# A transformer trunk on one core: new warm-up operands, the first chunk of x in halves, and weights rounded block by block in the opening

## The chip, the core and the metric

The kernel runs on one core of a Trainium2 chip. A core has a matrix engine (TensorE, PE in the profile, with its weight loads listed as PEld), three engines for other arithmetic (VectorE = DVE, ScalarE = ACT, GpSimd = POOL), an engine that mainly issues transfers (SyncE = SP), and 16 DMA engines, which move data between the chip's memory and the core's own memory. The metric is the device time of one execution in microseconds (us); a kernel's figure is the median of its runs.

## The reference

Two layers, sequence 512, width 1024, all in float32. Each layer: RMS norm, one combined input projection to 3072 columns, eight heads of stick-breaking attention and four of differential attention with rotary position, an output projection with residual add, RMS norm, and a squared-ReLU MLP of width 4096 with residual add. A final RMS norm ends it.

```python
h = rmsnorm(x, attn_norm[l])
proj = jnp.einsum('bsd,de->bse', h, w_in[l])
...
x = x + jnp.einsum('bse,ed->bsd', mixed, w_o[l])
h = rmsnorm(x, mlp_norm[l])
u = jnp.square(jax.nn.relu(jnp.einsum('bsd,df->bsf', h, w_ff1[l])))
x = x + jnp.einsum('bsf,fd->bsd', u, w_ff2[l])
```

## The kernel before

The activations lie transposed: `x` has 8 chunks (`KC`), chunk c with 128 features on the partitions and the 512 tokens along the row. The input projection's weights come in units of 128 columns, each a tile `raw` of 128x1024: 8 blocks of 128x128, block c belonging to chunk c.

Float32 accuracy is made from three products of rounded numbers. A value a is split into a rounded part and a rest, `hi` and `lo`, and a·b is taken as hi·hi + hi·lo + lo·hi. So each chunk costs three matmuls of 128x512 per unit. ACT makes the rounded part (L117 for weights, L250 for activations, there times the norm's gain), and DVE the rest (L133 and L251). The row factor 1/rms is applied later, to the results, so projections can begin before the norm is known.

The opening works on units 0 and 1 together (banks `p00` and `p01`, in the trace `p`), chunk by chunk, as the chunks of `x` and the blocks of the two weight tiles `raw0` and `raw1` arrive:

- ACT's queue fetches `begin` (L203: the gains and block 0 of `raw0`) and blocks 1 to 3 of `raw0` (L204).
- SP's queue fetches the chunks of `x` (L206) and, behind every second chunk, two blocks of `raw1` and, from chunk 4 on, two of `raw0` (L209). Later transfers reuse the completion semaphores of earlier ones: eight stand in a ring, so the ninth transfer of the program waits until the first has landed, the tenth until the second has, and so on.
- POOL fills the tile `edge` with zeros and an identity. PE runs eight warm-up matmuls of 128x512 in bf16 on the zeros (`WARM`, L223); their result is not used.
- `W.split_part(i, a, b)` rounds columns a to b of weight tile i; `make_h(c, g)` rounds chunk c. Block 0 of unit 0 is rounded on DVE (L116), all else on ACT.
- In `dense` (L785 to L803) PE works through chunk 0 with six matmuls at L792, chunk 1 with six at L796, and from chunk 2 on with the general three per unit and chunk (L300 to L302).

What runs in which order on one engine is decided when the program is built, by a scheduler that takes the code's order and its own estimate of when each operand is ready. `behind(a, b)` adds an edge: a is placed after b on its engine. Each engine then works strictly in that order, and a wait holds back all that is behind it. After the opening, four more units (`p0w`) follow on PE at once.

The lines by which the opening's rounding is ordered before the change:

```python
W.split_part(0, 0, P)
W.eager = False
opened = make_h(0, gcol("attn", 0, 0))
behind(opened[1], W.last[1])
W.split_part(1, 0, 2 * P)
...
W.split_part(0, P, 2 * P)
```

Of the kernel before, what the change touches and what calls it, by code (L numbers as in the profile page):

```python
# [9 lines left out]
F32 = mybir.dt.float32  # L10
F32R = mybir.dt.float32r
BF16 = mybir.dt.bfloat16
AF = mybir.ActivationFunctionType
# [4 lines left out]
P = 128  # L18
S = 512
# [146 lines left out]
def trunk(ctx, tc, opened, xT, w, w2, w1, gfin, lamv, cos, sin, out):  # L166
    nc = tc.nc
# [10 lines left out]
    def bank(tag, name):  # L178
        if tag == "any":
            tag = ("mm", "s", "s", "mm", "s")[turn[0] % 5]  # L180
            turn[0] += 1
        ring[0] += tag == "s"
        return ps.tile([P, 512], F32, tag=tag, name=name, bufs=banks[tag])
# [3 lines left out]
    W = _Weights(nc, w, wraw, wspl)  # L187
# [3 lines left out]
    x = cp.tile([P, KC, S], F32, tag="x", name="x")  # L191
# [7 lines left out]
    ident = edge[:, 384:512]  # L199
    lam_sm = cp.tile([P, L, 2], F32, tag="lamsm", name="lam_sm")  # L200
    lam_ex = cp.tile([P, L, 2], F32, tag="lamex", name="lam_ex")
    raws = [wraw.tile([P, 1024], F32, tag="raw", name=f"raw{i}") for i in range(2)]
    nc.scalar.dma_start(begin, opened)  # L203
    nc.scalar.dma_start(raws[0][:, P : 4 * P], w[0][:, P : 4 * P])  # L204
    for c in range(KC):
        nc.sync.dma_start(x[:, c, :], xT[c])  # L206
        if c % 2 == 0:
            for i in range(c < 4, 2):
                nc.sync.dma_start(raws[i][:, c * P : (c + 2) * P], w[i][:, c * P : (c + 2) * P])  # L209
    W.raw = dict(enumerate(raws))  # L210
    W.loaded = 2
    W.load(3)

    make_identity(nc, ident)
    mhalf = cp.tile([P, 4], F32, tag="mhalf", name="mhalf")
    nc.vector.memset(mhalf, -0.5)
    nc.gpsimd.memset(edge[:, 0:384], 0.0)
    prime = cp.tile([P, 1], F32, tag="prime", name="prime")
    nc.scalar.activation(prime, mhalf[:, 0:1], AF.Exp)
    zeros = edge.bitcast(BF16)  # L220
    pw = bank("t", "warm")
    for _ in range(WARM):
        nc.tensor.matmul(pw, zeros[:, 0:128], zeros[:, 128:640], start=True, stop=True)  # L223

    def gcol(which, l, c):
        i = {"attn": l * 8, "mlp": 16 + l * 8, "final": 32, "sub": 40 + l}[which] + c
        return g_all[:, i : i + 1]
# [18 lines left out]
            out=lo, in0=src, scalar=-1.0, in1=hi.bitcast(F32), op0=ALU.mult, op1=ALU.subtract)  # L246
        return a

    def make_h(c, g):
        a = nc.scalar.activation(h_hi[:, c, :], x[:, c, :], AF.Copy, scale=g)  # L250
        return a, nc.vector.scalar_tensor_tensor(  # L251
            out=h_lo[:, c, :], in0=x[:, c, :], scalar=g, in1=h_hi[:, c, :].bitcast(F32),
            op0=ALU.mult, op1=ALU.subtract)

    def add_sq(c, first, sqt, eng=nc.gpsimd):
# [6 lines left out]
    def behind(a, b):  # L262
        tc.add_manual_dep(a.ins, b.ins.name, mybir.DependencyInfo(
            mybir.DependencyClass.NoSync, mybir.DependencyReason.DATA), reason="order")
# [71 lines left out]
    for l in range(L):  # L336
        with ExitStack() as actx:
# [22 lines left out]
            if l == 0:  # L360
                W.eager = True
                W.split_part(0, 0, P)
                W.eager = False
                opened = make_h(0, gcol("attn", 0, 0))
                behind(opened[1], W.last[1])
                W.split_part(1, 0, 2 * P)
                for a, b in zip(W.last, opened):
                    behind(a, b)
                ahead = W.last
                W.split_part(0, P, 2 * P)  # L370
                for a, b in zip(W.last, ahead):
                    behind(a, b)
                for c in range(1, KC):
                    if c % 2 == 0:
                        for i in range(2):
                            W.split_part(i, c * P, (c + 2) * P)
                            if (c, i) == (2, 0):
                                for a, b in zip(W.last, opened):
                                    behind(a, b)
                    opened = make_h(c, gcol("attn", 0, c))  # L380
                    if c == 1:
                        for a, b in zip(opened, W.last):
                            behind(a, b)
                W.split = 2
            else:
                pts, halfway, opened = opened_by.pop()
# [399 lines left out]
            def dense(pts):  # L786
                if l == 0:
                    us = [W.next("x"), W.next("x")]
                    pts = [bank("mm", f"p{l}{i}") for i in range(2)]
                    for i, m in ((0, 0), (0, 2), (1, 0), (0, 1), (1, 1), (1, 2)):  # L790
                        a, b = wpair(us[i], 0), hpair(0)
                        nc.tensor.matmul(pts[i], a[m == 2], b[m == 1], start=m == 0, stop=False)  # L792
                    yield 6 * 0.216
                    for i, m in ((0, 0), (1, 0), (0, 2), (1, 2), (0, 1), (1, 1)):
                        a, b = wpair(us[i], 1), hpair(1)
                        nc.tensor.matmul(pts[i], a[m == 2], b[m == 1], start=False, stop=False)  # L796
                    yield 6 * 0.216
                    turns = [(c, i) for c in range(2, 5) for i in range(2)] + [(c, i) for i in range(2) for c in (5, 6, 7)]
                    for c, i in turns:
                        three(pts[i], wpair(us[i], c), hpair(c), False, c == KC - 1)  # L800
                        yield 3 * 0.216
                step, b = 2 * KC, int(ORDER[0][1])
                held = [(pts[0], "d", b, "q"), (pts[1], "d", b, "k")]  # L803
                def walk(name, kind, b, which):
                    if kind in "wu":
                        for _ in all_values() if kind == "w" else values_of(b):
                            yield None
                    else:
                        yield from block(name, "mm")

                for item in ORDER[1:]:
                    kind, b = item[0], int(item[1])
                    for which in ("qk" if kind in "ds" else "v"):
                        for pt in walk(f"p{l}{kind}{b}{which}", kind, b, which):
                            step += 1
                            if step == RA[l]:
                                rms_a(ssq, 1.0 / D, rcol, f"a{l}", last=W.product)
                            if step == RB[l]:
                                rms_b(rbc, f"a{l}", rcol)
                                nc.vector.tensor_mul(cos_t, cos_t, rbc)  # L820
                                nc.vector.tensor_mul(sin_t, sin_t, rbc)
                                for args in held:
                                    evict_d(*args)
                                held = []
                            yield 3 * 0.216
                        if kind in "ds":
                            {"s": evict_s, "d": evict_d}[kind](pt, kind, b, which)
                yield from wo(1)
# [551 lines left out]
```

## Time and profile before

| what | value |
|---|---|
| median of 3 runs | 1124.26 us (1123.91 to 1124.55) |
| the profiled execution's own time | 1124.27 us |
| its span, first instruction to last | 1122.5 us |
| PE busy | 1114.8 us, 99% of the span |
| DVE, ACT, POOL busy | 80%, 61%, 14% |

The rows shown further on have the start of an instruction and its length in us from the span's start, then engine, line, operation, tiles and shapes. In brackets stands how long its engine sat idle before it, and what ended that. `SPq` and `ACTq` rows are the issues of transfers; their length is that of the issue, not of the transfer. The lengths of matmuls are modelled and overlap, so the pace of PE is read from the distance between starts. In a row that merges several instructions (`x2`) only the first start is shown.

### The profile page before, as it was taken

To read this page: it belongs to the slowest core of one execution; us is meant where nothing else is said; L and a number is where in the kernel's file an instruction comes from. 1 tells how busy PE (TensorE), PEld (TensorE's weight loads), DVE (VectorE), ACT (ScalarE), POOL (GpSimd) and SP (SyncE) were. 2 spreads that over 40 slices of the span, in tenths; PEclk is the share of its full clock that TensorE was granted. 3 is DMA by queue.
4 is the path that set the end of the run, shared out by engine and by line. 5 is a ranking of instruction groups with operands and counts; after the bars stand their busy time and mean duration, and the time that the engine had idled before them with its cause. 6 is when DMAs were issued, how large, how long until landed. Compare 5 with 4: busy or idle time off the path is not lost.

```text
span 1122.5 us, 17199 instructions
## 1 busy us (share of the span) xinstructions
PE 1114.8 (99%) x6377; PEld 978.2 (87%) x6377; DVE 903.4 (80%) x1309; ACT 682.7 (61%) x1107; POOL 153.6 (14%) x233
## 2 busy tenths in 40 slices
PE   9999999999999999999999999999999999999997
PEld 7889889888899899899878898988888998998986
DVE  7788788798668779779877887887787787797787
ACT  6446666667558457467344566665774584674665
POOL 1001344101011001001000014430011010010010
PEclk9999999999999999999999999999999999999999
DMA  7466343268687678658325654512676786787462
GB/s 249 137 191 184 112 133 114 73 220 232 172 217 169 182 200 185 189 134 211 109 75 148 197 146 130 168 59 76 209 175 183 202 189 175 184 185 206 113 132 94
DMA packets 61043, 181.25 MB, mean 161 GB/s; under 512 B 7456, under 2 KB 8736, under 8 KB 60960
## 3 DMA queue, kind: packets, MB, share of 16 engines
q1 hardware_dynamic: 50160, 141.84, 40.0%
q0 software_dynamic: 10368, 37.75, 19.2%
q8 instruction: 50, 0.82, 0.3%
q10 hardware_dynamic: 432, 0.56, 0.1%
q14 instruction: 33, 0.27, 0.1%
HBM read 150.77 MB, written 4.19 MB: 138 GB/s over the span
## 4 chain that ended last, share of the span: by engine, by line
PE 98%; DVE 1%; issue 0%; POOL 0%; ACT 0%; POOLq 0%; DVEq 0%
PE X L300 9%; PE X L302 9%; PE X L301 9%; PE V L300 4%; PE V L302 4%; PE V L301 4%; PE wo L300 3%; PE wo L301 3%; PE wo L302 3%; PE f L300 3%; PE f L302 3%; PE f L301 3%; PE Y L300 2%; PE Y L302 2%; PE Y L301 2%; PE W L302 1%
## 5 line engine op out<-in xcount | busy, mean ns | idle before, releaser
L117 ACT ACTIVATE whi<-q 128x1024 fp32r<-128x1024 f32 x96 | 101.7, 1059 | 108.5 <-PE X L302 38.1
L133 DVE TENSOR_TENSOR wlo<-q,whi 128x1024 fp32r<-128x1024 f32 x96 | 117.1, 1222 | 46.5 <-ACT whi L117 46.3
L133 DVE TENSOR_TENSOR wlo<-raw,whi 128x1024 fp32r<-128x1024 f32 (+1 forms) x82 | 97.2, 1191 | 11.0 <-ACT whi L117 11.0
L117 ACT ACTIVATE whi<-raw 128x1024 fp32r<-128x1024 f32 (+1 forms) x82 | 80.8, 993 | 37.6 <-issue 8.9
L300 PE MATMUL X<-whi,Ah 128*128 128x512 f32 x248 | 97.7, 394 | 0.0
L301 PE MATMUL X<-wlo,Ah 128*128 128x512 f32 x248 | 96.8, 390 | 0.0
L302 PE MATMUL X<-whi,Al 128*128 128x512 f32 x248 | 96.7, 390 | 0.0
L133 DVE TENSOR_TENSOR wlo<-waves,whi 128x1024 fp32r<-128x1024 f32 x40 | 48.9, 1221 | 16.5 <-ACT whi L117 16.4
L117 ACT ACTIVATE whi<-waves 128x1024 fp32r<-128x1024 f32 x40 | 42.2, 1055 | 29.7 <-PE X L302 20.5
L300 PEld LDWEIGHTS X<-whi,Ah 128*128 128x128 f32 x248 | 46.6, 188 | 12.0 <-DVE y L1104 1.9
L302 PEld LDWEIGHTS X<-whi,Al 128*128 128x128 f32 x248 | 46.6, 188 | 9.9
L302 PE MATMUL X<-hxh,wlo 128*128 128x256 f32 x192 | 54.4, 283 | 0.0
L302 PE MATMUL X<-h_hi,wlo 128*128 128x256 f32 x192 | 54.4, 283 | 0.0
L301 PE MATMUL X<-hxl,whi 128*128 128x256 f32 x192 | 54.4, 283 | 0.0
L301 PE MATMUL X<-h_lo,whi 128*128 128x256 f32 x192 | 54.4, 283 | 0.0
L300 PE MATMUL X<-hxh,whi 128*128 128x256 f32 x192 | 54.4, 283 | 0.0
L301 PEld LDWEIGHTS X<-wlo,Ah 128*128 128x128 f32 x248 | 46.6, 188 | 8.9
L300 PE MATMUL X<-h_hi,whi 128*128 128x256 f32 x192 | 54.4, 283 | 0.0
L300 PE MATMUL f<-h_hi,whi 128*128 128x512 f32 x128 | 50.4, 394 | 0.0
L302 PE MATMUL f<-h_hi,wlo 128*128 128x512 f32 x128 | 49.9, 390 | 0.0
L301 PE MATMUL f<-h_lo,whi 128*128 128x512 f32 x128 | 49.9, 389 | 0.0
L240 DVE TENSOR_TENSOR Al<-x,Ah 128x512 fp32r<-128x512 f32 (+1 forms) x60 | 46.5, 792 | 3.8 <-ACT Ah L239 3.5
(712 smaller groups left out, 3702.6 us busy)
## 6 DMA issues: line engine op xcount, KB each, us to landing
raw<-in_w SPq DMA_DIRECT2D x78, 512.0 KB, 3.6
q<-in_w SPq DMA_DIRECT2D x48, 512.0 KB, 4.6
q<-in_w POOLq DMA_DIRECT2D x48, 512.0 KB, 7.6
waves<-in_w SPq DMA_DIRECT2D x28, 512.0 KB, 4.5
first_a<-in_w SPq DMA_DIRECT2D x12, 512.0 KB, 4.7
first_b<-in_w SPq DMA_DIRECT2D x12, 512.0 KB, 5.2
first_c<-in_w SPq DMA_DIRECT2D x12, 512.0 KB, 4.3
first_b<-in_w POOLq DMA_DIRECT2D x12, 512.0 KB, 6.7
```

The costliest lines, as they stand in the source:

```text
L117: return self.nc.scalar.activation(o, src, AF.Copy)
L133: self.last = h, nc.vector.tensor_tensor(out=lo[:, a:b], in0=raw[:, a:b], in1=hi[:, a:b].bitcast(F32), op=ALU.subtract)
L240: nc.vector.tensor_tensor(out=lo, in0=src, in1=hi.bitcast(F32), op=ALU.subtract)
L300: nc.tensor.matmul(pt, ah, bh, start=first, stop=False, skip_group_check=goes_on),
L301: nc.tensor.matmul(pt, ah, bl, start=False, stop=False, skip_group_check=goes_on),
L302: nc.tensor.matmul(pt, al, bh, start=False, stop=last, skip_group_check=goes_on))
```

## The change

Four things are changed, all in the opening.

- The warm-up matmuls read one column of `mhalf` as both operands, repeated over 128 and 512 columns by a step of zero. `mhalf` is filled by DVE with -0.5; the lower half of that float, read as bf16, is zero. So the result is again zero, and the warm-up waits for that fill instead of POOL's.
- Chunk 0 of `x` is fetched in two halves of 256 tokens, and `make_h` rounds it half by half. The first two products of unit 0 (`whi` and `wlo` with the rounded `x`) are made as two matmuls of 256 columns each.
- Block 0 of `raw1` is fetched alone, on ACT's queue between `begin` and the blocks of `raw0`; its block 1 follows on SP's queue.
- The weights of the first two chunks are rounded block by block, in the order unit 1 block 0, unit 0 block 1, unit 1 block 1; before, both blocks of unit 1 went in one instruction.

There are two transfers more (three on ACT's queue instead of two, one more on SP's opening list), three more ACT instructions in name (an issue among them), two more on DVE, and two more matmuls. POOL's list is unchanged. On PE a few products of the last chunks and of `p0w` change places; behind `p0w` the lists of all engines are as before.

On ACT, from the first rounding on, before:

```order
L250 ACTIVATE h_hi<-x,begin 128x512 [waits DMAHW1_49,DMAHW0_49]
L117 ACTIVATE whi_151<-raw_80 128x256 [waits DMAHW3_49]
L117 ACTIVATE whi_145<-raw_79 128x128 [waits DMAHW2_49]
L250 ACTIVATE h_hi<-x,begin 128x512 [waits DMAHW4_49]
L117 ACTIVATE whi_145<-raw_79 128x256
L250 ACTIVATE h_hi<-x,begin 128x512 [waits DMAHW5_49]
L117 ACTIVATE whi_151<-raw_80 128x256 [waits DMAHW6_49]
L250 ACTIVATE h_hi<-x,begin 128x512 [waits DMAHW7_49]
```

and on ACT at the same place now (`raw_79` is `raw0`, `raw_80` is `raw1`):

```order
L254 ACTIVATE h_hi<-x,begin 128x256 [waits DMAHW1_49,DMAHW0_49]
L254 ACTIVATE h_hi<-x,begin 128x256 [waits DMAHW3_49]
L117 ACTIVATE whi_155<-raw_80 128x128 [waits DMAHW2_49]
L117 ACTIVATE whi_147<-raw_79 128x128 [waits DMAHW4_49]
L117 ACTIVATE whi_155<-raw_80 128x128 [waits DMAHW5_49]
L254 ACTIVATE h_hi<-x,begin 128x512 [waits DMAHW6_49]
L117 ACTIVATE whi_147<-raw_79 128x256
L117 ACTIVATE whi_155<-raw_80 128x256 [waits DMAHW0_49]
L254 ACTIVATE h_hi<-x,begin 128x512 [waits DMAHW7_49]
L254 ACTIVATE h_hi<-x,begin 128x512 [waits DMAHW1_49]
```

Beside the halves and the single blocks, the rounding of `raw1`'s blocks 2 and 3 has moved: it stood behind the rounding of chunk 2, and now stands ahead of it.

On SP's queue, from the program's start, before:

```order
L206 DMA x<-in_xT 128x512
L209 DMA raw_80<-in_w 128x256
L206 DMA x<-in_xT 128x512 x2
L209 DMA raw_80<-in_w 128x256
L206 DMA x<-in_xT 128x512
L206 DMA x<-in_xT 128x512 [waits DMAHW0_49]
L209 DMA raw_79<-in_w 128x256 [waits DMAHW1_49]
L209 DMA raw_80<-in_w 128x256 [waits DMAHW2_49]
```

and now (`DMAHW0` is the semaphore of `begin`):

```order
L208 DMA x<-in_xT 128x256 x2
L212 DMA raw_80<-in_w 128x128
L208 DMA x<-in_xT 128x512 x2
L212 DMA raw_80<-in_w 128x256 [waits DMAHW0_49]
L208 DMA x<-in_xT 128x512 [waits DMAHW1_49]
L208 DMA x<-in_xT 128x512 [waits DMAHW2_49]
L212 DMA raw_79<-in_w 128x256 [waits DMAHW3_49]
L212 DMA raw_80<-in_w 128x256 [waits DMAHW4_49]
```

With two transfers more ahead, the first that must wait for `begin` is no longer chunk 4 of `x`, but blocks 2 and 3 of `raw1`, with chunk 3 behind it.

On PE, the matmuls of chunk 2, before:

```order
L300 MATMUL p_235<-h_hi,whi_145 128x512 [waits Activation_49]
L301 MATMUL p_235<-h_lo,whi_145 128x512 [waits DVE_49]
L302 MATMUL p_235<-h_hi,wlo_146 128x512
L300 MATMUL p_236<-h_hi,whi_151 128x512 [waits Activation_49]
L301 MATMUL p_236<-h_lo,whi_151 128x512
L302 MATMUL p_236<-h_hi,wlo_152 128x512 [waits DVE_49]
```

and now:

```order
L304 MATMUL p_241<-h_hi,whi_147 128x512 [waits Activation_49]
L304 MATMUL p_242<-h_hi,whi_155 128x512
L305 MATMUL p_241<-h_lo,whi_147 128x512 [waits DVE_49]
L306 MATMUL p_241<-h_hi,wlo_148 128x512
L305 MATMUL p_242<-h_lo,whi_155 128x512
L306 MATMUL p_242<-h_hi,wlo_156 128x512
```

The first product with `h_lo` is now the third of the chunk, not the second.

The diff, with what the prediction speaks of:

```diff
     nc.scalar.dma_start(begin, opened)
+    nc.scalar.dma_start(raws[1][:, 0:P], w[1][:, 0:P])
     nc.scalar.dma_start(raws[0][:, P : 4 * P], w[0][:, P : 4 * P])
     for c in range(KC):
-        nc.sync.dma_start(x[:, c, :], xT[c])
+        for t in ([slice(0, 256), slice(256, S)] if c == 0 else [slice(0, S)]):
+            nc.sync.dma_start(x[:, c, t], xT[c][:, t])
         if c % 2 == 0:
             for i in range(c < 4, 2):
-                nc.sync.dma_start(raws[i][:, c * P : (c + 2) * P], w[i][:, c * P : (c + 2) * P])
+                a = max(c, 1) * P
+                nc.sync.dma_start(raws[i][:, a : (c + 2) * P], w[i][:, a : (c + 2) * P])
...
-    make_identity(nc, ident)
     mhalf = cp.tile([P, 4], F32, tag="mhalf", name="mhalf")
     nc.vector.memset(mhalf, -0.5)
+    make_identity(nc, ident)
...
+    nought = mhalf.bitcast(BF16)[:, 0:1]
     for _ in range(WARM):
-        nc.tensor.matmul(pw, zeros[:, 0:128], zeros[:, 128:640], start=True, stop=True)
+        nc.tensor.matmul(pw, nought.to_broadcast([P, P]), nought.to_broadcast([P, S]), start=True, stop=True)
...
-    def make_h(c, g):
-        a = nc.scalar.activation(h_hi[:, c, :], x[:, c, :], AF.Copy, scale=g)
+    def make_h(c, g, t=slice(0, S)):
+        a = nc.scalar.activation(h_hi[:, c, t], x[:, c, t], AF.Copy, scale=g)
...
-                opened = make_h(0, gcol("attn", 0, 0))
-                behind(opened[1], W.last[1])
-                W.split_part(1, 0, 2 * P)
-                for a, b in zip(W.last, opened):
-                    behind(a, b)
-                ahead = W.last
-                W.split_part(0, P, 2 * P)
-                for a, b in zip(W.last, ahead):
-                    behind(a, b)
+                halves = [slice(0, 256), slice(256, S)]
+                for t in halves:
+                    ahead, opened = W.last, make_h(0, gcol("attn", 0, 0), t)
+                    behind(opened[1], ahead[1])
+                    W.last = opened
+                for i, c in ((1, 0), (0, 1), (1, 1)):
+                    ahead = W.last
+                    W.split_part(i, c * P, c * P + P)
+                    for a, b in zip(W.last, ahead):
+                        behind(a, b)
...
-                        nc.tensor.matmul(pts[i], a[m == 2], b[m == 1], start=m == 0, stop=False)
+                        for t in halves if (i, m) in ((0, 0), (0, 2)) else [slice(0, S)]:
+                            nc.tensor.matmul(pts[i][:, t], a[m == 2], b[m == 1][:, t], start=m == 0 and not t.start, stop=False)
```

More of the change, by code (lines that the diff above doesn't have):

```diff
@@ L247, in split_less @@
         return a
-    def make_h(c, g):
-        a = nc.scalar.activation(h_hi[:, c, :], x[:, c, :], AF.Copy, scale=g)
+    def make_h(c, g, t=slice(0, S)):
+        a = nc.scalar.activation(h_hi[:, c, t], x[:, c, t], AF.Copy, scale=g)
         return a, nc.vector.scalar_tensor_tensor(
-            out=h_lo[:, c, :], in0=x[:, c, :], scalar=g, in1=h_hi[:, c, :].bitcast(F32),
+            out=h_lo[:, c, t], in0=x[:, c, t], scalar=g, in1=h_hi[:, c, t].bitcast(F32),
             op0=ALU.mult, op1=ALU.subtract)
```

## The prediction

> **What bounds the kernel now.** I read the page first: busy shares, then the chain of waits.
>
> ```profile
> span 1122.5 us, 17199 instructions
> PE 1114.8 (99%) x6377; PEld 978.2 (87%) x6377; DVE 903.4 (80%) x1309; ACT 682.7 (61%) x1107; POOL 153.6 (14%) x233
> PE 98%; DVE 1%; issue 0%; POOL 0%; ACT 0%; POOLq 0%; DVEq 0%
> ```
>
> PE carries 98% of the chain that ended last. A change in the opening is worth the time by which PE ends the opening earlier or later; behind it nothing is idle that could swallow a shift, so I carry it to the end one to one. Second, the chain of the first 18 us, in order of time (start, length):
>
> ```profile
> 0.88 0.43 POOL edge L217
> 1.36 3.59 PE warm L223 x8
> 4.95 2.63 PE p L792 x6
> 7.58 1.37 PE p L796 x6
> 8.96 0.23 PE p L300
> ```
>
> The warm-up ends at 4.95, and from there PE does not wait once. Six products of chunk 0 take 2.63 us, six of chunk 1 only 1.37. Third, the timeline of PE shows why, and that of ACT, DVE and SP what PE starts on:
>
> ```profile
> 4.93 0.29 PEld L792 LDWEIGHTS p<-h_hi,whi 128*128 128x128 f32 x1 [0.88 <-ACT h_hi L250]
> 5.53 0.63 PE L792 MATMUL p<-h_hi,wlo 128*128 128x512 f32 x1
> 5.95 0.63 PE L792 MATMUL p<-h_hi,whi 128*128 128x512 f32 x1
> 6.38 0.97 PE L792 MATMUL p<-h_lo,whi 128*128 128x512 f32 x2
> 7.19 0.40 PE L792 MATMUL p<-h_hi,wlo 128*128 128x512 f32 x1
> 7.42 0.63 PE L796 MATMUL p<-h_hi,whi 128*128 128x512 f32 x2
> 8.79 0.39 PE L300 MATMUL p<-h_hi,whi 128*128 128x512 f32 x1
> 9.02 0.39 PE L301 MATMUL p<-h_lo,whi 128*128 128x512 f32 x1
> ...
> 0.82 0.06 DVE L216 MEMSET mhalf<- 128x4 f32 x1 [0.82 <-PEq L1369]
> 4.16 0.72 ACT L250 ACTIVATE h_hi<-x,begin 128x512 fp32r<-128x512 f32 x1 [0.99 <-DMA begin<-in_opened]
> 4.78 0.60 ACT L117 ACTIVATE whi<-raw 128x256 fp32r<-128x256 f32 x2
> 5.55 0.72 ACT L250 ACTIVATE h_hi<-x,begin 128x512 fp32r<-128x512 f32 x1 [0.17 <-DMA x<-in_xT]
> 6.76 0.72 ACT L250 ACTIVATE h_hi<-x,begin 128x512 fp32r<-128x512 f32 x1 [0.18 <-DMA x<-in_xT]
> 7.39 0.40 ACT L117 ACTIVATE whi<-raw 128x256 fp32r<-128x256 f32 x1
> 7.75 1.37 ACT L250 ACTIVATE h_hi<-x,begin 128x512 fp32r<-128x512 f32 x2
> 7.51 0.75 DVE L251 SCALAR_TENSOR_TENSOR h_lo<-x,begin,h_hi 128x512 fp32r<-128x512 f32 x1
> ...
> 2.60 0.43 SPq L209 DMA_DIRECT2D raw<-in_w  x1
> 4.15 0.33 SPq L206 DMA_DIRECT2D x<-in_xT  x1
> ```
>
> Starts 5.53, 5.95, 6.38 are 0.43 apart; 7.19 and 7.42 are 0.23 apart. So TensorE runs at about half pace until some point between 6.81 and 7.19, warm-up included (8 in 3.59 us), though the clock column reads full here:
>
> ```profile
> 5.00:6.00 1.00, 1.00 (x3) 0.81 (x4) 1.00 (x3) 0.83 (x3) 0.00 (x0) 1.00 0.90 314
> 6.00:7.00 1.00, 1.00 (x4) 0.81 (x3) 0.90 (x3) 0.82 (x3) 0.00 (x0) 1.00 1.06 396
> 7.00:8.00 1.00, 1.00 (x6) 0.81 (x5) 0.87 (x3) 1.00 (x3) 0.00 (x0) 1.00 1.05 382
> ```
>
> In these stretches the seventh number is that column (1.00), the eighth the DMA engines' busy share, the last GB/s: the transfers run at the DMA engines' limit. The first product streams from 5.53 - 0.43 = 5.10, behind 0.17 us of its weight load.
>
> **The change part by part.**
>
> *Warm-up.* PE started 0.06 after the last fill of `edge` (0.88 + 0.43 = 1.31, start 1.36). With `mhalf` it starts at 0.82 + 0.06 + 0.06 = 0.94, 0.42 earlier, and ends at 4.53. The first real product then waits for its operand; the 0.42 is no gain by itself. What it could move is the change of pace. Bounds: it comes 0.42 earlier too, and 0.42 × (1 - 0.23/0.43) = 0.20 is gained; or it falls later by as much, and 0.20 is lost. One execution doesn't tell what it is tied to; I take 0. The Trainium skill, "TensorE: Matmul & The Clock Gate", Part 1, says that the release follows activity windows of about 3.4 us that run freely and do not begin with the kernel. Here it came 5.5 to 5.8 us after the first matmul, between one such window and two, which agrees; one run can't show that they run freely. By that page the sum keeps 0 on average and moves by a few tenths from run to run; if instead pace were tied to the first matmul, the sum would be 0.20 better.
>
> *Chunk 0 in halves.* ACT's nearest row is L1005, the same operation on 128x256; its minimum, median and maximum in ns:
>
> ```profile
> L1005 ACT ACTIVATE x<-x,begin x8: 492/495/512, 241.9 to 810.0; 128x256 f32<-128x256 f32 x8
> ```
>
> It takes 0.50 for 0.72, so the first half is ready at 4.16 + 0.50 = 4.66, and PE streams from 5.10 - 0.23 = 4.87. The second half: ACT began its next instruction 0.62 after a 512 (4.16 to 4.78), so 0.62 - 0.23 = 0.39 after a 256; it ends at 4.16 + 0.39 + 0.50 = 5.05, and PE has it at 5.10. Warm products of 256 columns start 0.12 apart:
>
> ```profile
> 96.24 0.28 PE L440 MATMUL p0u<-whi,h_lo 128*128 128x256 f32 x1
> 96.36 0.28 PE L438 MATMUL p0u<-whi,h_hi 128*128 128x256 f32 x1
> ...
> 5.53 0.33 PEld L792 LDWEIGHTS p<-h_hi,whi 128*128 128x128 f32 x1
> ```
>
> The first two rows show half of 0.23 and no more, so at the slow pace I take 0.43/2 = 0.21 each: first half 4.87 to 5.08, second 5.10 to 5.31, the two of `wlo` to 5.74, where the second product ended at 5.95. Gain 0.2. Bounds: `begin` now shares the DMA engines with half a chunk at first, up to 0.13 MB less at the 0.39 MB per us shown above, 0.3 earlier, gain 0.5; or the weight load of each half shows at the slow pace (0.33 in the third row, over a product of 0.21), 3 × 0.12 = 0.36 lost, net 0.15 worse. I take 0.2, by the rows of 256 columns.
>
> *Blocks one by one.* The rows of the issue on ACT's queue and of the rounding, in ns:
>
> ```profile
> L204 ACTq DMA_DIRECT2D raw<-in_w x1: 451/451/451, 1.2 to 1.2; - x1
> L117 ACT ACTIVATE whi<-raw x8: 293/400/403, 4.8 to 11.3; 128x256 fp32r<-128x256 f32 x7, 128x128 fp32r<-128x128 f32 x1
> ```
>
> ACT issues one rounding more: 0.29 + 0.29 for 0.40, and the halves cost 2 × 0.50 for 0.72, 0.45 more in all; overlapped as in the rows above, about 0.3. ACT waited 0.17 for chunk 1 and 0.18 for chunk 2, which takes it up. DVE has the same extra beside a wait. Unit 1 block 0 is rounded by about 5.3 and first used at 5.74; chunk 1's `h_lo`, which ended at about 7.05, moves by up to 0.2 and is used at 8.34 - 0.2. Cost 0. `raw0`'s blocks are issued 0.45 later on ACT's queue, behind the new transfer; block 1 is needed first by the third product of chunk 1, near 7.7. Cost 0.
>
> *SP's queue.* The new order makes `raw1` blocks 2 and 3 wait for `begin`, so they are issued at 4.15 and not at 2.60, and chunk 3 behind them. The landings, by the transfers issued in two stretches (KB each, us from issue to landing):
>
> ```profile
> raw<-in_w SPq DMA_DIRECT2D x1, 128.0 KB, 4.5
> x<-in_xT SPq DMA_DIRECT2D x1, 256.0 KB, 4.2
> DMA to landing us min/median/max: 3.2/4.2/4.7
> ```
>
> Now: 2.60 + 4.5 = 7.1. The transfer issued at 4.15 lands at 8.35; between the two 512 KB land, 0.52 MB at 0.39 MB per us = 1.3 us. So landings go by bytes ahead, not by the time of issue, and as many bytes stand ahead of `raw1` as before (the third row is for chunks of `x`). Its landing is bounded by 7.1 (place in the queue kept), 4.15 + 3.2 = 7.35 (the shortest lag of a chunk, which has twice the bytes), and 4.15 + 4.5 = 8.65. I take 7.1.
>
> *Order on ACT.* The rounding of these blocks now stands ahead of chunk 2. It starts at about 7.13, chunk 2 follows 0.36 later (7.39 to 7.75) at 7.49 and not 6.76, and ends at 8.21; DVE begins its rest 0.03 later and needs 0.75: 8.99. Chunk 2 begins on PE at 8.79 - 0.2 = 8.59 (rounded part there at 8.21), and its third product, now the first with `h_lo`, at 8.59 + 2 × 0.23 = 9.05. So a slack of about 0.8 (8.26 against 9.02 before) goes down to 0.06, and no stall is in the sum. Later chunks have it better: each costs PE 6 × 0.23 = 1.36 and ACT and DVE about 1.1 with the weights.
>
> Sum: 0 - 0.2 + 0 + 0 = -0.2 us against the profiled execution's 1124.27 (its span 1122.5 and 1.8 around it), which is the median of the runs to 0.01. That is 1124.1, and 0.02% of the time, far below 0.2%, about what a measurement of this kernel can tell from no change.
>
> **The rivals.**
>
> *A new wait in ACT's order (slower).* If the later issue does delay `raw1`, chunk 2 waits behind it. With the landing at 8.65, its rounded part ends at 9.76 and its rest at 10.54. PE stalls at 8.59 until 9.8 (1.2), then at the third product from 10.27 to 10.57 (0.3): 1.5 - 0.2 = 1.3 worse, 1125.6. It decides from a landing of 7.16 on; at 7.35 it costs 0.2 and cancels the gain. For it: the slack is gone. Against: the landings above go by bytes.
>
> *The gain is lost.* The extra weight loads show, or the slack of 0.06 is overdrawn: 1124.3 to 1124.6.
>
> *The pace changes earlier.* 0.2 more is gained on PE, but `h_lo` of chunk 2 stays at 8.99, so the new order gives back all but 0.06: 1124.0. Where in addition transfers land 0.3 earlier, 1123.6.
>
> *The step-zero operand is slow.* No matmul in this trace streams a repeated column; the nearest load a repeated column as weights and show nothing odd:
>
> ```profile
> L293 PEld LDWEIGHTS rb_a<-edge,rcol x8: 133/136/137, 28.1 to 582.9; 128*128 128x128 f32 x8
> ```
>
> If each warm-up product took twice 0.43, they would end at 0.94 + 7.2 = 8.1, 3.2 later: 1127.3, slower by 0.3%.
>
> **How the numbers follow.** Forecast 45%, gain lost 22%, earlier pace 12%, new wait 16%, slow operand 4%, anything else 1%. Predicted 1124.1. The range runs from 1123.5 (earlier pace with earlier landings) to 1125.0 (a landing of `raw1` up to about 8.1); outside are the slow operand, the harsher half of the new wait, and a few per cent below. Beyond 2.25 us on the slow side lies only the slow operand, so slower 4%; a gain of 2.25 us would need PE to skip more than chunk 0's whole loss at the slow pace, 2.63 - 1.37 = 1.26: 1%. Within 0.2%: 95%.
>
> **What the profile of the changed kernel would show.** The warm-up starts near 0.95, at distances of 0.43. The first product's weight load waits for ACT until about 4.7, the second half starts near 5.1, the first product of unit 1 near 5.75. `raw1` blocks 2 and 3 are issued at about 4.15 and land near 7.1; ACT's second chunk starts near 7.5. On PE the third product of chunk 2 starts near 9.05, with no wait or one below 0.1. I am wrong if a wait for ACT or DVE of several tenths stands at chunk 2, if the warm-up's distances are not 0.43, or if anything behind 20 us waits that did not.

## The result and the profile after

| | before | after |
|---|---|---|
| median of 22 runs | 1124.28 us (1123.76 to 1126.17) | 1125.83 us (1125.06 to 1126.84) |
| profiled execution | 1124.27 us, span 1122.5 | 1125.86 us, span 1124.0 |

The ratio is 1.0014, with a 95% interval of 1.0008 to 1.0019: 1.55 us (0.14%) slower, above the predicted range (1123.5 to 1125.0), and against the forecast 1124.1.

One execution of e12, below, ran at a granted clock of 0.65 throughout and took 1575.4 us; the figures given for e12 are of its other eleven.

PE's counted busy time is 0.7 longer and its idle time 0.8 longer. The lengths of matmuls are modelled, so the place of the loss is read from their starts:

```profile
span 1124.0 us, 17211 instructions
PE 1115.5 (99%) x6379; PEld 977.8 (87%) x6379; DVE 903.6 (80%) x1311; ACT 683.3 (61%) x1109; POOL 153.9 (14%) x233
```

In the timeline of the changed kernel (start, length; in brackets the idle time ahead and what ended it), PE's rows with one of DVE and one of PE's weight loads:

```profile
3.50 0.23 DVE L116 CAST whi<-begin 128x128 fp32r<-128x128 f32 x1 [2.63 <-DMA begin<-in_opened]
0.94 3.59 PE L227 MATMUL warm<-mhalf 128*128 128x512 bf16 x8 [0.94 <-DVE mhalf L218]
4.10 0.98 PE L798 MATMUL p<-h_hi,whi 128*128 128x256 f32 x2
4.88 0.63 PE L798 MATMUL p<-h_hi,wlo 128*128 128x256 f32 x2
...
6.32 0.40 PE L798 MATMUL p<-h_hi,wlo 128*128 128x512 f32 x1
7.82 0.74 PE L802 MATMUL p<-h_hi,whi 128*128 128x512 f32 x2 [1.10 <-ACT h_hi L254]
...
9.32 0.63 PE L304 MATMUL p<-h_hi,whi 128*128 128x512 f32 x2
9.95 0.19 PEld L305 LDWEIGHTS p<-h_lo,whi 128*128 128x128 f32 x1 [0.44 <-DVE h_lo L255]
9.95 0.50 PE L305 MATMUL p<-h_lo,whi 128*128 128x512 f32 x1
```

The front half went better than forecast. The first product began at 4.10 (4.93 before), the last of chunk 0 at 6.32 (7.19 before): PE was 0.87 ahead. `begin` had landed at 3.48 (DVE's row starts on it), 0.65 earlier than before. Then PE waited for chunk 1 and began it at 7.82 (7.42 before): 0.40 behind, a loss of 1.27 in one place. ACT and SP show on what:

```profile
4.35 0.29 ACT L117 ACTIVATE whi<-raw 128x128 fp32r<-128x128 f32 x1
6.56 0.51 ACT L117 ACTIVATE whi<-raw 128x128 fp32r<-128x128 f32 x2 [1.91 <-DMA raw<-in_w]
7.05 0.72 ACT L254 ACTIVATE h_hi<-x,begin 128x512 fp32r<-128x512 f32 x1
7.67 0.82 ACT L117 ACTIVATE whi<-raw 128x256 fp32r<-128x256 f32 x2
8.40 1.94 ACT L254 ACTIVATE h_hi<-x,begin 128x512 fp32r<-128x512 f32 x3
...
3.50 0.33 SPq L212 DMA_DIRECT2D raw<-in_w  x1
3.87 0.91 SPq L208 DMA_DIRECT2D x<-in_xT  x2
4.83 2.06 SPq L212 DMA_DIRECT2D raw<-in_w  x2
```

ACT had its work for chunk 0 done at 4.64 and stood for 1.91 until a transfer landed. After's transfers that were issued between 1.6 and 2.4 us, and then before's that bring the same data (issued between 1.1 and 1.7), each with its KB and the time from issue to landing:

```profile
x<-in_xT SPq DMA_DIRECT2D x1, 256.0 KB, 4.9
raw<-in_w ACTq DMA_DIRECT2D x1, 192.0 KB, 4.9
raw<-in_w SPq DMA_DIRECT2D x1, 64.0 KB, 4.7
```

```profile
x<-in_xT SPq DMA_DIRECT2D x1, 256.0 KB, 3.9
raw<-in_w ACTq DMA_DIRECT2D x1, 192.0 KB, 3.7
raw<-in_w SPq DMA_DIRECT2D x1, 128.0 KB, 3.3
```

The 64 KB of `raw1`'s block 1, issued at 1.66, took 4.7 us and landed at 6.4; before, blocks 0 and 1 together, issued at 1.19, had landed at 4.5. `raw0`'s blocks 1 to 3 landed at 6.5 instead of 4.9, and chunk 1 of `x`, issued at 2.13, at 7.0 instead of 1.66 + 3.9 = 5.5; ACT began to round it at 7.05. The same bytes stand ahead of chunk 1 in both kernels (928 KB with its own). So it is the flow that sagged. The windows of before, then of after (the last three numbers: granted clock, busy share of the DMA engines, GB/s):

```profile
3.40:3.80 0.40, 0.40 (x2) 0.15 (x1) 0.00 (x0) 0.00 (x0) 0.00 (x0) 1.00 1.06 370
3.80:4.20 0.40, 0.40 (x2) 0.15 (x1) 0.04 (x1) 0.04 (x1) 0.00 (x0) 1.00 1.17 359
4.20:4.60 0.40, 0.40 (x2) 0.00 (x0) 0.40 (x4) 0.40 (x1) 0.00 (x0) 1.00 0.95 328
4.60:5.00 0.40, 0.40 (x2) 0.07 (x1) 0.20 (x2) 0.40 (x2) 0.00 (x0) 1.00 1.29 328
```

```profile
2.80:3.40 0.60, 0.60 (x3) 0.15 (x1) 0.00 (x0) 0.60 (x1) 0.00 (x0) 1.00 1.06 342
3.40:3.80 0.40, 0.40 (x2) 0.15 (x1) 0.29 (x4) 0.39 (x3) 0.00 (x0) 1.00 0.81 160
3.80:4.20 0.40, 0.40 (x3) 0.10 (x1) 0.38 (x3) 0.40 (x2) 0.00 (x0) 1.00 0.64 113
4.20:4.60 0.40, 0.40 (x3) 0.29 (x2) 0.40 (x2) 0.40 (x2) 0.00 (x0) 1.00 0.88 122
4.60:5.00 0.40, 0.40 (x3) 0.40 (x3) 0.40 (x2) 0.05 (x1) 0.00 (x0) 1.00 0.51 165
```

From 2.8 to 3.4 after moves 342 GB/s. Then, for 1.6 us, it moves 140 on average where before moved 346: 0.33 MB less, which is 0.95 us at before's rate; the rest of chunk 1's 1.5 is not accounted for by this.

It is not the accident of one execution. In three profiles with before's transfers (before, e1, e2) chunk 1 landed at 5.5 and the flow from 3.4 to 4.6 was 328 to 379 GB/s; in the four with after's (after, e3, e7, e11) chunk 1 landed at 7.0 to 7.5 and the flow was 95 to 195.

It does not end with chunk 1. SP's issue of a later `raw1` transfer stood from 5.4 to 6.55 behind a semaphore that `raw0`'s late landing had to free (the row of 4.83, 2.06 long for two issues), so chunk 7 of `x` landed at 13.9 instead of 11.7, and the squares' sum on DVE, and with it `rs_a` on PE, came late. The last addition of that sum began at 22.78, before at 20.52, as much later as chunk 7 had landed. `rs_a` reads this sum, which was done at 23.46 (its bracket names what DVE began just then):

```profile
22.78 0.68 DVE L264 TENSOR_TENSOR norms<-norms,sq 128x512 f32<-128x512 f32 x1
23.61 0.63 PE L275 MATMUL rs_a<-edge,norms 128*128 128x128 f32 x4 [0.21 <-DVE lam_pr L330]
```

Counted product by product, PE stands 0.87 ahead at the end of chunk 0, 0.40 behind at chunk 1's first, 0.85 behind from the end of chunk 2 on, and 1.25 behind after `rs_a`; another 0.3 is lost in waits near 160 us.

### The profile page after: what moved, and what is told of

Same layout as the page of the kernel before. It is cut to its first block, busy times and chain, and to the rows that moved or that the text cites. A ratio compares the mean times of both kernels' runs of the same rounds, so it can differ in the third digit from the quotient of the medians.

```text
span 1124.0 us, 17211 instructions
## 1 busy us (share of the span) xinstructions
PE 1115.5 (99%) x6379; PEld 977.8 (87%) x6379; DVE 903.6 (80%) x1311; ACT 683.3 (61%) x1109; POOL 153.9 (14%) x233
## 4 chain that ended last, share of the span: by engine, by line
PE 95%; DVE 2%; DMA 1%; issue 1%; ACT 1%; POOL 1%; SPq 0%; ACTq 0%; POOLq 0%; DVEq 0%
PE X L304 9%; PE X L305 9%; PE X L306 9%; PE V L304 4%; PE V L305 4%; PE V L306 4%; PE wo L304 3%; PE wo L306 3%; PE wo L305 3%; PE f L304 3%; PE f L306 3%; PE f L305 3%; PE Y L305 2%; PE Y L304 2%; PE Y L306 2%; PE W L305 1%
## 5 line engine op out<-in xcount | busy, mean ns | idle before, releaser
L133 DVE TENSOR_TENSOR wlo<-raw,whi 128x1024 fp32r<-128x1024 f32 (+2 forms) x83 | 97.3, 1180 | 12.5 <-ACT whi L117 12.5
L117 ACT ACTIVATE whi<-raw 128x1024 fp32r<-128x1024 f32 (+2 forms) x83 | 81.1, 984 | 39.5 <-issue 8.9
```

What stands on the lines that cost most here:

```text
L117: return self.nc.scalar.activation(o, src, AF.Copy)
L133: self.last = h, nc.vector.tensor_tensor(out=lo[:, a:b], in0=raw[:, a:b], in1=hi[:, a:b].bitcast(F32), op=ALU.subtract)
```

## The experiments

All were timed against the kernel before on the same chip. Differences are of medians in us; one run's interval is about 1 us wide to either side, so a single row below 1 is not told from nothing by itself.

| run | kernel | median (range) | before there | difference | ratio, 95% |
|---|---|---|---|---|---|
| e1 | before + new warm-up operands | 1123.96 (1123.52 to 1125.80) | 1124.16 | -0.2 | 0.9994 to 1.0011 |
| e2 | after, transfers as before | 1124.32 (1123.42 to 1125.83) | 1124.16 | +0.2 | 0.9995 to 1.0013 |
| e3 | before + after's transfers | 1125.39 (1124.63 to 1126.62) | 1124.16 | +1.2 | 1.0004 to 1.0021 |
| e4 | before + two transfers of 4 KB | 1124.51 (1124.28 to 1125.07) | 1124.16 | +0.4 | 0.9996 to 1.0013 |
| e5 | after, chunk 0 fetched whole | 1125.03 (1124.24 to 1125.88) | 1123.94 | +1.1 | 0.9999 to 1.0017 |
| e6 | after, `raw1` fetched as before | 1124.63 (1123.34 to 1126.17) | 1123.94 | +0.7 | 0.9996 to 1.0015 |
| e7 | after, chunk 2 first on ACT | 1125.78 (1125.17 to 1127.23) | 1123.94 | +1.8 | 1.0007 to 1.0025 |
| e8 | before + two transfers of 0.5 KB | 1124.61 (1124.05 to 1125.94) | 1123.94 | +0.7 | 0.9998 to 1.0015 |
| e9 | before + four transfers of 4 KB | 1125.42 (1125.14 to 1127.83) | 1124.05 | +1.4 | 1.0007 to 1.0025 |
| e10 | e2 with one transfer fewer | 1125.24 (1124.23 to 1125.84) | 1124.05 | +1.2 | 0.9999 to 1.0017 |
| e11 | after + five idle matmuls | 1125.94 (1124.98 to 1126.52) | 1124.05 | +1.9 | 1.0008 to 1.0025 |
| e12 | e1 with nine warm-ups | 1124.17 (1123.83 to 1124.62) | 1123.98 | +0.2 | 0.9993 to 1.0011 |
| e13 | e10 with ten warm-ups | 1124.89 (1124.62 to 1125.39) | 1123.98 | +0.9 | 0.9999 to 1.0016 |

**Which part costs: e1, e2, e3**

e1, the warm-up alone:

```diff
+    nought = mhalf.bitcast(BF16)[:, 0:1]
     for _ in range(WARM):
-        nc.tensor.matmul(pw, zeros[:, 0:128], zeros[:, 128:640], start=True, stop=True)
+        nc.tensor.matmul(pw, nought.to_broadcast([P, P]), nought.to_broadcast([P, S]), start=True, stop=True)
```

> The kernel before, with the new warm-up operands alone; all transfers, roundings and products as before. Transfer-count theory (each transfer of 128 rows takes about 0.41 us of a stage that all queues share before its data can flow, whatever its size, so two more transfers push all later data back): the warm-up starts at about 0.94 and nothing else moves; within 0.3 us of before. Warm-up theory (the earlier start or the repeated column spoils the pace of PE): 0.8 to 1.5 us slower. Order theory (rounding block by block, with unit 1's blocks 2 and 3 ahead of chunk 2 on ACT): within 0.3 us.

e2, everything but the transfers (against after):

```diff
-    nc.scalar.dma_start(raws[1][:, 0:P], w[1][:, 0:P])
...
-        for t in ([slice(0, 256), slice(256, S)] if c == 0 else [slice(0, S)]):
-            nc.sync.dma_start(x[:, c, t], xT[c][:, t])
+        nc.sync.dma_start(x[:, c, :], xT[c])
...
-                a = max(c, 1) * P
-                nc.sync.dma_start(raws[i][:, a : (c + 2) * P], w[i][:, a : (c + 2) * P])
+                nc.sync.dma_start(raws[i][:, c * P : (c + 2) * P], w[i][:, c * P : (c + 2) * P])
```

> The changed kernel with the transfers of before: chunk 0 of x in one, blocks 0 and 1 of unit 1 in one on SP's queue. Warm-up, rounding by halves and by blocks and the products by halves stay. Transfer-count theory: chunk 1 lands at about 5.5 again, PE starts at about 4.7, 0 to 0.4 us faster than before. Order theory: slower by 0.5 to 1.5 us. Warm-up theory: slower by 0.8 to 1.5 us.

e3, the same lines the other way round in before: after's transfers, nothing else.

> The kernel before with the changed kernel's transfers alone: x's chunk 0 in halves, unit 1's block 0 alone on ACT's queue. Warm-up, roundings and products as before. Transfer-count theory: chunk 1 lands near 7.0 and not 5.5, 1.0 to 1.8 us slower than before. Order theory and warm-up theory: within 0.3 us of before.

The warm-up alone and everything but the transfers both stay at before's time; the transfers alone cost 1.2 of the 1.55. In e3 the warm-up, the rounding and the products are before's, and the sag of the flow is there, with the same lag of the 64 KB (its windows and the landing of the transfer issued at 1.66):

```profile
3.40:3.80 0.40, 0.40 (x2) 0.15 (x1) 0.23 (x3) 0.24 (x2) 0.00 (x0) 1.00 0.51 158
3.80:4.20 0.40, 0.40 (x2) 0.15 (x1) 0.32 (x3) 0.20 (x1) 0.00 (x0) 1.00 0.46 127
...
raw<-in_w SPq DMA_DIRECT2D x1, 64.0 KB, 4.6
```

In e2 the same stretches moved 379 and 365 GB/s. So most of the loss lies in the transfers (e3's profile is one of its faster executions, 1124.91, and shows PE 0.65 behind after the opening). But e2 doesn't keep its early start either: in its profile PE is 0.92 ahead at chunk 1's first product and, as chunk 2 lands at 7.25 (6.73 before, with the same transfers), 0.29 ahead at chunk 3's first; after `rs_a` it is 0.19 behind. e1 also shows that step-zero operands run at the usual 0.43.

**One split at a time: e5, e6**

e5 takes back the halves of chunk 0, e6 the single block of `raw1` (the pieces of e2's diff, one each).

> The changed kernel with chunk 0 of x fetched in one again (still rounded and multiplied in halves); unit 1's block 0 stays alone on ACT's queue. If the loss of 1.3 to 1.6 us comes from both extra transfers alike, about half of it stays: 0.4 to 1.0 us slower than before, chunk 1 landing near 6.3. If it is all the half chunks' doing (rows of 1024 bytes for 2048), within 0.3 us of before. If it is all the single block's doing (rows of 512 bytes), as slow as the changed kernel.

> The changed kernel with blocks 0 and 1 of unit 1 fetched in one on SP's queue again; chunk 0 of x stays in halves. Both alike: 0.4 to 1.0 us slower than before, chunk 1 landing near 6.3. All by the half chunks: as slow as the changed kernel. All by the single block: within 0.3 us of before. On ACT the rounding of chunk 2 stands ahead of unit 1's blocks 2 and 3 here, as before the change.

Each has one transfer more than before. Neither shows the deep sag: e5 moved 388 and 378 GB/s from 3.4 to 4.2 us,

```profile
3.40:3.80 0.40, 0.40 (x2) 0.15 (x1) 0.00 (x0) 0.24 (x2) 0.00 (x0) 1.00 1.23 388
3.80:4.20 0.40, 0.40 (x2) 0.00 (x0) 0.24 (x3) 0.24 (x1) 0.00 (x0) 1.00 1.10 378
```

and e6 361 and 270. Chunk 1 landed at 5.8 in e5 and at 6.1 in e6, between before's 5.5 and after's 7.0. Their medians lie between before and after, with intervals that reach no change. In these two executions, then, one split alone doesn't bring the deep sag. Each is the third fastest of its eleven (1124.38 and 1123.80), so that the slower ones lack it too is not shown, and how the loss divides between the splits these runs cannot say.

**ACT's order: e7**

This is the place of the prediction's slower rival. Chunk 2's rounding is put ahead of that of `raw1`'s blocks 2 and 3, as before the change:

```diff
+                    if c == 2:
+                        for a, b in zip(W.last, opened):
+                            behind(a, b)
```

> The changed kernel with one edge more, which puts the rounding of unit 1's blocks 2 and 3 behind chunk 2 on ACT and DVE, as before the change. In the changed kernel's profile chunk 2 had landed by 7.72 and its rounding began at 8.40; PE waited 0.44 for its rest. If that order carries part of the loss, this wait goes and the time is 0.3 to 0.5 us below the changed kernel, near 1125.4. If the late transfers alone carry it, the wait turns up at unit 1's blocks or at chunk 3 instead, and the time stays within 0.2 us of the changed kernel's 1125.8.

No gain shows: 1.8 above before, where after is 1.55 above; with the interval of one run a few tenths either way stay open. The larger wait is at chunk 1, ahead of this place. Its profiled execution (1127.16) showed something else. Chunk 1 was late enough for PE to stand idle for over 2 us, and the clock fell:

```profile
8.29 1.20 PE L805 MATMUL p<-h_hi,whi 128*128 128x512 f32 x2 [2.06 <-ACT h_hi L254]
9.28 1.05 PE L805 MATMUL p<-h_hi,wlo 128*128 128x512 f32 x2
...
8.00:9.00 1.00, 0.71 (x2) 0.62 (x3) 0.73 (x2) 1.00 (x3) 0.00 (x0) 0.67 0.92 328
9.00:10.00 1.00, 1.00 (x4) 0.81 (x3) 1.00 (x4) 1.00 (x4) 0.00 (x0) 0.50 1.06 287
10.00:11.00 1.00, 1.00 (x4) 0.71 (x4) 1.00 (x4) 1.00 (x4) 0.00 (x0) 0.50 0.91 288
11.00:12.00 1.00, 1.00 (x4) 0.84 (x3) 1.00 (x4) 1.00 (x3) 0.00 (x0) 0.62 1.15 238
```

The granted clock is 0.50 from about 8.34 (0.67 in its stretch) to about 11.76 (0.62): 3.4 us. The Trainium skill, "TensorE: Matmul & The Clock Gate", Part 1, gives activity windows of about 3.4 us that run freely; the length agrees. Its section "Why this matters for your kernels" warns of idle gaps above about 3 us; here a wait of 2.06 was enough.

**What of a transfer costs: e4, e8, e9, e10**

e4 adds to before two transfers that nothing reads, of 128 rows of 32 bytes; e8 the same with 16 rows; e9 four as in e4.

```diff
     nc.scalar.dma_start(begin, opened)
+    nc.scalar.dma_start(extra[:, 8:16], w[1][:, 8:16])
...
         nc.sync.dma_start(x[:, c, :], xT[c])
+        if c == 0:
+            nc.sync.dma_start(extra[:, 0:8], w[1][:, 0:8])
```

> The kernel before with two transfers of 128 rows of 32 bytes more, into a tile that nothing reads: one on ACT's queue behind begin, one on SP's behind chunk 0. 8 KB more in all. Transfer-count theory: the first rows of chunk 1 come about 0.8 us later, time 0.5 to 1.5 us slower than before. Small-row theory (the loss comes from moving the same bytes in rows of 512 and 1024 bytes, that is from the DMA engines' own rate): within 0.3 us of before, since no row of the real data has become smaller.

> The kernel before with the two small extra transfers of the run with two small ones, but of 16 rows each and not 128. If the cost of a transfer goes by its rows, it is an eighth of 0.41 us here: the first weights of unit 1 land at about 4.7 and chunk 1 at about 5.6, and the time is that of before within 0.2 us. If each transfer costs the same whatever its rows, they land near 5.5 and 6.3 as there, and the time is 0.2 to 0.5 us above before.

> The kernel before with four transfers more that nothing reads, each of 128 rows of 32 bytes: two on ACT's queue behind `begin`, two on SP's behind chunk 0 of `x`. With two of them (e4) blocks 0 and 1 of `raw1` landed at 5.54 and chunk 1 of `x` at 6.35, against 4.54 and 5.52 before. If each transfer costs a fixed time of a stage that all queues share (about 0.41 us): twice the shift, `raw1` at 6.3 to 6.6 and chunk 1 at 7.1 to 7.4, PE's wait at chunk 1 grows by 0.8, and the time is 1124.9 to 1125.6. If the stage is one that works ahead and is only short at the start: the shift stays at that of e4, and the time at 1124.2 to 1124.6. If the cost is that of bytes: nothing moves (32 KB in all are 0.1 us), 1124.1 to 1124.3.

In e4 `raw1`'s blocks 0 and 1 and `raw0`'s (issued at 1.66) took

```profile
raw<-in_w ACTq DMA_DIRECT2D x1, 192.0 KB, 4.0
raw<-in_w SPq DMA_DIRECT2D x1, 128.0 KB, 3.9
```

and landed at 5.5 and 5.7, 1.0 and 0.8 later than before, for 8 KB more. In e8 it was 5.9 and 6.1, for 1 KB more. In both, 0.47 of this is that they are issued later, behind the added transfer of their queue; their time from issue to landing grew by 0.5 and 0.3 in e4, and by 0.9 and 0.7 in e8. With an eighth of the rows and bytes the cost is no smaller, so neither sets it. Little of it shows in e4's time (+0.4), since before's chunk 1 had landed 1.9 us ahead of its first product (5.5 and 7.42).

e9 then broke the simple form of this, a fixed time for each transfer. With four, `raw1` and `raw0`, issued 0.47 later than in e4, took

```profile
raw<-in_w ACTq DMA_DIRECT2D x1, 192.0 KB, 3.5
raw<-in_w SPq DMA_DIRECT2D x1, 128.0 KB, 3.4
```

and landed at 5.5 and 5.7 again: as long after their issue as before (3.3 and 3.7 there), so that all of their delay is the later issue, two times 0.47. The second pair added nothing to the landing here. What e9 loses it loses in the ring: with four transfers more, chunk 1 of `x` became the ninth and waited on SP for `begin` to land:

```profile
4.05 0.81 SPq L208 DMA_DIRECT2D x<-in_xT  x2
8.12 0.73 PE L801 MATMUL p<-h_hi,whi 128*128 128x512 f32 x2 [0.52 <-ACT h_hi L255]
```

it was issued at 4.05 instead of 1.66 and landed at 7.3, and PE began chunk 1 at 8.12. The chunks behind it came late likewise; product by product, PE leaves the opening 1.5 behind, close to the loss in time (1.4).

e10 goes the other way: block 0 of `raw1` is carried in `begin`, and blocks 1 to 3 come in one transfer.

```diff
-    begin = cp.tile([P, 192], F32, tag="begin", name="begin")
+    begin = cp.tile([P, 320], F32, tag="begin", name="begin")
...
+            a, b = {0: (1, 4), 2: (0, 0)}.get(c, (c, c + 2))
+            for i in range(c < 4, 2 * (b > 0)):
+                nc.sync.dma_start(raws[i][:, a * P : b * P], w[i][:, a * P : b * P])
```

> The changed kernel (new warm-up operands, halves and single blocks in the rounding and the products), with `x` whole, block 0 of `raw1` carried in `begin` beside block 0 of `raw0`, and blocks 1 to 3 of `raw1` in one transfer behind chunk 0: one transfer fewer than before, three fewer than the changed kernel, the same bytes in all. If the count of transfers sets the pace at the start: chunk 2 of `x` lands by about 0.4 earlier than before's 6.73, PE meets no wait that before has not, and the time is 1123.6 to 1124.1, below that of e2's kernel (1124.32) by 0.2 to 0.6. If bytes alone set it: chunk 1 lands at before's time plus 0.17 for the 64 KB that now stand ahead of it, and the time is that of e2's kernel, 1124.2 to 1124.5.

It was no better than e2's kernel: 1125.24, 1.2 above its before (e2: 0.2; the intervals overlap), so neither reading held. The flow had no sag where after's has it (355 and 337 GB/s from 3.4 to 4.2 us), which fits the count; but `begin` with 160 KB landed at 4.4, chunk 1, with 128 KB more ahead of it, at 6.5 instead of 5.5, and PE stood between warm-up and first product and stayed near half pace past 8.76 (two products from there to 9.53), where before had the full pace from 7.19:

```profile
4.99 0.98 PE L796 MATMUL p<-h_hi,whi 128*128 128x256 f32 x2 [0.46 <-DVE wlo L133]
...
8.76 0.93 PE L800 MATMUL p<-h_hi,wlo 128*128 128x512 f32 x2
9.53 0.63 PE L800 MATMUL p<-h_lo,whi 128*128 128x512 f32 x2
```

**The clock: e11, e12, e13**

e11 bridges PE's wait at chunk 1 of the changed kernel with five matmuls on zeros; e12 is e1 with `WARM = 9`, e13 is e10 with `WARM = 10`.

```diff
+                        for _ in range(5 if (i, m) == (0, 0) else 0):
+                            idle = nc.tensor.matmul(pw, nought.to_broadcast([P, P]), nought.to_broadcast([P, S]), start=True, stop=True)
+                            behind(idle, last)
+                            last = idle
```

> The changed kernel with five more matmuls of the warm-up's kind (zero times zero, result unused) on PE between the products of chunk 0 and those of chunk 1, where PE otherwise waits about 1.1 us for `raw0` and chunk 1. They take some 1.1 us at the full pace, so PE hardly pauses there. If pauses at that place make the clock fall back in some executions, and that lifts the median: the runs above 1126.4 are gone and the median is 1125.2 to 1125.6. If the clock has no part in the median: 1125.6 to 1126.0, as the changed kernel, or up to 0.2 more, where the five delay chunk 1's first product.

> The kernel of e1 (before with the new warm-up operands alone) with nine warm-up matmuls instead of eight. In e1 the eighth ended at 4.5, the first product began at 4.71, and the full pace was there at 5.42; two of its eleven runs stood at 1125.4 and 1125.8, the others at 1123.5 to 1124.6. If a hole in PE's work between warm-up and first product puts the full pace off by a window of 3.4 us in some runs: the ninth closes the hole, no run is above 1124.8, and the median is 1123.6 to 1123.9. If those two runs are due to something else: one to three of eleven stay above 1125, median 1123.9 to 1124.2.

> The kernel of e10 with ten warm-up matmuls instead of eight. In e10 `begin` (160 KB) landed at 4.41, the first product began at 4.99 after an idle 0.46, and the full pace came at 9.40, the latest of all profiles; thirteen products ran at 0.43 instead of 0.23 until then. If that hole is why e10 was slow: the two fill it, the full pace comes between 4.3 and 7.8, and the median falls to 1123.9 to 1124.5. If the transfers are why (chunk 1 of `x` landed at 6.55, before 5.52): the median stays at 1124.9 to 1125.5.

e11: the five ran from 5.95 on and cut PE's idle time ahead of chunk 1 to 0.84, and the median didn't fall (1.9 above before, after 1.55):

```profile
5.95 1.27 PE L803 MATMUL warm<-mhalf 128*128 128x512 bf16 x5
8.05 0.73 PE L806 MATMUL p<-h_hi,whi 128*128 128x512 f32 x2 [0.84 <-ACT h_hi L254]
```

After's profiled execution, 1125.86 and so at its median, had no falling clock at all. So a falling clock doesn't make the median loss. e12's eleven runs all lie below 1124.7, where e1 had two of eleven above 1125.4; that fits the hole in PE's work, but two runs prove little, and the median is no better. e13 stands 0.9 above before, e10 1.2, a difference within the intervals; its range is 0.8 us wide, e10's 1.6. In e13's profile PE begins chunk 1 at 7.40, as before, and then waits 0.53 at chunk 2, which landed at 7.7 (6.7 before).

The traces have a closer pair for the hole. In after and in e10 the warm-up began at 0.94; after's full pace came at 5.99, e10's at 9.40, 3.4 later, which is also the length of e7's stretch at half clock. In the 3.4 us ahead of 5.99, e10 has the 0.46 of idle PE in front of its first product and after has none. So in this pair the hole goes with a full pace that is one such stretch late; two executions are no proof of it. No kernel here was shown to beat the kernel before.

**What stays open.** What makes the flow sag when two small transfers are added is not shown. It comes at different places: the lowest flow was 140 GB/s from 4.6 to 5.0 us in e8, 88 from 3.4 to 3.8 in e9. The views name no engine or queue that is full. e4, e8 and e9 say that bytes and rows are not it, and that beyond the 0.47 of its issue a transfer has no fixed price. Each of them adds transfers to both queues, so they can't say whether one on one queue delays the other.

## Why the prediction was wrong

- *Warm-up, 0*: it starts at 0.94 with distances of 0.43, as forecast, and e1 stays at before's time; its interval (0.7 below to 1.2 above) can't tell 0 from the bounds of 0.20.
- *Chunk 0 in halves, -0.2*: PE got ahead by 0.87, but not by the step in the sum. `begin` landed at 3.48 instead of 4.13, 0.65 earlier, where the bound said 0.3. The first product with `wlo` began at 4.88 instead of 5.53, 0.65 earlier too: from the landing of `begin` it is 1.40 in both, so the halves of the rounding gained nothing in this execution. The other 0.22 is the pace: from that product to the last of chunk 0 PE took 1.44 (4.88 to 6.32), before 1.66 (5.53 to 7.19), since the full pace came earlier in this execution. None of it lasted: the next operand was not there.
- *Blocks one by one*, "`raw0`'s blocks are issued 0.45 later on ACT's queue, behind the new transfer; [...] Cost 0": this step failed. The lag from issue to landing was carried over from the other kernel, so the added transfers were costed at the time of their issue alone. They landed 1.65 later, not 0.45, block 1 of `raw1` 1.8 later, and chunk 1 1.5 later. PE lost 1.27 there. The landing of chunk 1 was never put to the test: the rivals look for a wait at chunk 2 alone. And block 1 of `raw0` is an operand of chunk 1's first product, not of its third.
- *SP's queue*, "landings go by bytes ahead, not by the time of issue, and as many bytes stand ahead of `raw1` as before": the rule failed. It had been read off a stretch at 0.39 MB per us, and taken for one in which after's transfers moved at 113 to 165 GB/s. `raw1`'s blocks 2 and 3 landed at 8.05, not 7.1, though issued at 3.50 and not at 4.15; in e4, 8 KB in two transfers moved landings by 0.8 to 1.0. Some of it is scatter that one profile couldn't show: with before's transfers these blocks landed at 6.8 in e1, 7.1 in before and 7.6 in e2.
- *Order on ACT*: the slack of 0.06 at chunk 2's third product was indeed overdrawn, and that product began at 9.95 instead of 9.05, behind a wait of 0.44 for DVE: the sign of error that was named for chunk 2. But this is the smaller part (0.40 behind at chunk 1 to 0.85 behind), and e7, with the order taken back, shows no gain.
- The rival *a new wait in ACT's order* gave 1125.6, near the measured time, for the wrong reason: it had the late landing, but at chunk 2 and from the late issue alone. *Earlier pace* came in the profiled execution (the 0.22 above) and was lost with the rest; *the gain is lost* had the overdrawn slack, but not the size of the loss (1124.3 to 1124.6); *slow operand* did not come.
- *No wait behind 20 us that was not there*: named as a sign of error, and it came: `rs_a`, 0.4, by chunk 7's landing 2.26 later, which SP's wait for the ring and the lost bytes bring. In e2, with before's transfers, PE lost as much there.
- The Trainium skill's windows (the page named in the prediction): the fall in e7 lasted 3.4 us, which agrees. The full pace came between 3.4 us (e11) and 8.5 us (e10) after the first matmul, so it isn't tied to that matmul; one profile can't give the sum a term for it.

## What to carry to other kernels

Where a stage starts on data that is still arriving, splitting a transfer can bring its first part earlier and what stands behind it later: here chunk 0's first half and `begin` landed about 0.7 earlier, and chunk 1 landed 0.25 and 0.5 later with one split each (e5, e6) and 1.5 later with both. Before splitting, write down the landing and first use of every transfer behind it, not only of the one that is split. Count transfers as well as bytes: in the first few microseconds two more, one on each queue, made the next landings 0.8 to 1.4 us later here, even at 0.5 KB each, and each also moves the point at which a ring of completion semaphores makes a queue wait. An early start of the engine that bounds the kernel is worth only the smallest slack that follows it: after's 0.87 and e2's 0.92 were both gone before 25 us.

## What the runs showed of the hardware that was not expected

- Two added transfers of 0.5 KB each (16 rows of 32 bytes) moved the landing of the next ones on both queues by 1.2 to 1.4 us (e8: 5.9 and 6.1 for 4.5 and 4.9), of which 0.47 is the later issue; four of 4 KB moved them by 0.8 to 1.0, no more than the later issue (e9).
- With after's transfers the DMA engines moved 113 to 165 GB/s from 3.4 to 5.0 us, where with before's they moved 328 to 370.
- A half clock came back in the middle of work after a wait of about 2 us, for 3.4 us (e7).
- A matmul that streams one column repeated with a step of zero, as weights and as data, runs at the usual distance of 0.43 at half pace (e1).
